# An encoder layer with expert-choice routing on one core: a half-width first gather, another order in the weight ring, and dummy matmuls

## The chip, the cores and the metric

The kernel runs on one NeuronCore of a Trainium2 chip. The metric is the device time of one execution in microseconds (us). Five engines work beside each other, each through its own queue and in order: TensorE (PE in the profile; PEld are its weight loads), VectorE (DVE), ScalarE (ACT), GpSimd (POOL) and SyncE (SP). SP issues nearly all DMA transfers here.

## What is computed

The reference is one layer of an encoder over 512 tokens of width 1024. Three token mixers (neighbourhood attention, grouped-query attention and attention to 256 memory tokens) are gated, added and normalized. Then comes a mixture of 16 experts, in which each expert chooses 64 tokens:

```python
cap = EC_CAPACITY_FACTOR * T // N_EXPERTS          # 64
aff = jax.nn.softmax(x @ w_router, axis=-1)
gate, idx = lax.top_k(jnp.swapaxes(aff, 1, 2), cap)
xs = x[bidx, idx]
h = jnp.einsum('becd,edf->becf', xs, w_gate_up)
hg, hu = jnp.split(h, 2, axis=-1)
ye = jnp.einsum('becf,efd->becd', jax.nn.silu(hg) * hu, w_down)
ye = ye * gate[..., None]
y = jnp.zeros_like(x).at[bidx, idx].add(ye)
out = layer_norm(DN_ALPHA * x + y, ln2_g, ln2_b)
```

All weights are float32. An expert has 12 MB of them, and each is used once.

## The kernel before, in words

The instructions of each engine stand in the order in which the Python code writes them; no scheduler moves them. A tile is allocated under a tag. The next tile of the same tag waits for the readers of the one before, also those written later.

**First half.** Weights of the mixers come in 74 units of 128 x 1024. Each is split into a high and a low part (`hi_lo`, L86 to L88: ScalarE rounds, VectorE subtracts), and three matmuls replace one. The first unit comes together with the memory tokens in four parts; `first_unit` (L288) does two high products of each part as soon as ScalarE is done, then four products with the low parts of VectorE. `k_item` (L308) calls it for h = 0 and then does the second unit in the same way (`t_piece`, L269 to L271: with k = 0 its third product is the first that needs the low part of the weights). Nine dummy matmuls on an identity (L234) run before.

**Routing.** After the last projection the router's logits are sorted per expert (`rounds`, L1093 and L1096), the cut is found (`cut`, `dg`, `thp` at L1170), positions come from `cnp` (L1179 to L1185). `keep_warm(n)` (L1113) issues n dummies; the call with 28 stands ahead of the sort's last part (L1156).

**Gather.** For a group of four experts, `onehot` (L1194) compares positions with 1 to 64 and gives a 512 x 256 one-hot (64 slots for each of the four experts). `gather` (L1208) multiplies the tokens, split in XH and XL, by it: for each of 8 feature blocks f, 8 matmuls with weights from XH or XL (L1216, L1218) and 256 moving columns, evacuated by VectorE (f even, L1223) or ScalarE (f odd, L1221). After the eighth step come the gate values gw (L1232) in the bank of tag Y, which has one buffer, and their reductions on VectorE (L1239). Before expert 0 three steps run, the others stand between the products of expert 0.

**Experts.** `gate_up` (L1245) multiplies the 64 gathered tokens by the two halves of a unit gu(e,k), k = 0 to 7; `h_transpose` (L1268) and `down` (L1277) use dn(e,k), k = 0 to 3. The loop over experts (L1526 on) does the first four gu of expert e, then dn of expert e-1, then the other four gu. In expert 2 `residual` (L1325) puts the tokens into the accumulator acc, in steps between the products: the first two steps, on VectorE (L1332), are written right after gu(2,0), four more (L1336, L1342) up to gu(2,2). Then comes the copy of hT(1) (L1275), without which the y product of expert 1 (L1287) can't start. acc has the tag G1.

**The ring.** A unit of expert weights has 1 MB. `RING` (L32) lists twelve blocks of one or two units, each in the buffer of a tag. `_blocks` (L40) puts the units, in the order of use, into blocks: first all twelve, then again and again the ten that are not in `ONCE` (raw and G1). Blocks 0 to 6 are loaded during the first half; blocks 7 to 9 (G1, Q6, Q9) wait for the last projection's operands, block 10 (M) for the token tile's last reader, block 11 (VS) for `cnp`. When the last unit of a block is used, `done` (L813) asks for the next block on SP's queue, whose request waits for TensorE's readers of that tag. Before the change Q6 holds dn(0,3) and gu(1,4), Q9 gu(1,5) and gu(1,6), M gu(1,7) and gu(2,0), VS gu(2,1), and G1 dn(0,1) and dn(0,2). Blocks 12 to 23 then go to Q2, Q1, Q5, Q7, Q4, Q3, Q6, Q9, M, VS, Q2, Q1; 23 follows in the buffer of dn(1,0) and dn(1,1).

Of the kernel before, what the change touches and what calls it, by code (L numbers as in the profile page):

```python
# [28 lines left out]
NEG = -1e30  # L29
RSQRT_SEED = float(0x5F3759DF)  # L30
N_UNITS = 74
RING = (("Q2", 2), ("Q1", 2), ("Q5", 2), ("Q7", 2), ("Q4", 2), ("Q3", 2), ("raw", 1), ("G1", 2), ("Q6", 2), ("Q9", 2), ("M", 2),  # L32
        ("VS", 1))
ONCE = ("raw", "G1")
N_SINGLE = 10
# [4 lines left out]
def _blocks():  # L40
    order = []
    for e in range(NEXP - 1):
        order += [("gu", e, k) for k in range(4)]
        if e:
            order += [("dn", e - 1, k) for k in range(4)]
        order += [("gu", e, k) for k in range(4, KD)]
    order += [("gu", NEXP - 1, k) for k in range(KD)]
    order += [("dn", e, k) for e in (NEXP - 2, NEXP - 1) for k in range(4)]
    again = [t for t in RING if t[0] not in ONCE]
    blocks, i = [], 0  # L50
    while i < len(order):
        b = len(blocks)
        tag, n = RING[b] if b < len(RING) else again[(b - len(RING)) % len(again)]
        blocks.append((tag, n, order[i:i + n], i + n > len(order) - N_SINGLE))
        i += n
    return blocks
# [3 lines left out]
def layer_kernel(ctx: ExitStack, tc: tile.TileContext, xt, xn, first0, wu, bgate, rpb, gains, wrt,  # L60
# [134 lines left out]
    def first_part(t, k, o, n):  # L195
        return t[:, k // 2, o + (k % 2) * n:o + (k % 2) * n + n]
# [81 lines left out]
    def n_chunk(acc, us, ah, al, m, hooks={}):  # L278
        c = slice(m * P, (m + 1) * P)
        for k in range(KD):  # L280
# [4 lines left out]
            nc.tensor.matmul(acc, ah[:, k, c], lo, start=False, stop=False)  # L285
            nc.tensor.matmul(acc, al[:, k, c], h, start=False, stop=(k == KD - 1))

    def first_unit(acc):  # L288
        for i in range(4):
            ks = (2 * i, 2 * i + 1)  # L290
            for k in ks:
                nc.tensor.matmul(acc, first_part(fh, k, 512, P), memh[:, k], start=(k == 0), stop=False)
            for k in ks:
                nc.tensor.matmul(acc, first_part(fh, k, 512, P), meml[:, k], start=False, stop=False)
                nc.tensor.matmul(acc, first_part(fl, k, 512, P), memh[:, k], start=False, stop=(k == KD - 1))
# [3 lines left out]
    def g_mem():  # L299
        zz = R("Q3", [P, 4, 1024], "mkvzs")  # L300
        ST["A5"] = zz[:, 0:2]
        ST["A6"] = zz[:, 2:4]
        mk = ST["A5"][:, 0].rearrange("p (h t) -> p h t", h=4)
        mv = ST["A6"][:, 0].rearrange("p (m f) -> p m f", m=2)
        qm = R("Q2", [P, 4, S], "qmT")
        ST.update(mkT=mk, mv=mv, qmT=qm)

        def k_item(h):  # L308
            u, = ws.take()
            ws.prefetch()  # L310
            acc = PB("mm", f"mk{h}")
            if h == 0:
                first_unit(acc[:, :256])
            else:
                t_unit(acc[:, :256], u, memh, meml)
            if h >= 2:
                split_x(h - 2)
            yield
            nc.vector.tensor_copy(mk[:, h], acc[:, :256])

        def q_item(h):
            u, = ws.take()
            ws.prefetch()
            acc = PB("mm", f"qm{h}")
            t_unit(acc, u, xh, xl)
            yield
            nc.scalar.activation(qm[:, h], acc, AF.Copy, scale=1.0 / math.sqrt(128.0))

        def v_item(q):
            us = ws.take(2)  # L330
            for m in range(2):
                acc = PB("mm", f"mv{q}{m}")
                n_chunk(acc[:, :256], us, memh, meml, m)
                ws.prefetch(1 + m)
                if q == 0:
                    split_x(2 + m)
                yield
                nc.scalar.copy(mv[:, m, q * 256:(q + 1) * 256], acc[:, :256])

        for h in range(4):  # L340
            yield from k_item(h)
        for q in range(2):
            yield from v_item(q)
        for h in range(4):
            yield from q_item(h)
# [807 lines left out]
    for m in (2, 3):  # L1153
        x1_norm(m)
        x1_parts(m)
    keep_warm(28)  # L1156
    ring.upto(len(RING))
    dump("aff", aff)

# [31 lines left out]

    OH, XS, GW = {}, {}, {}

    def onehot(qd):  # L1194
        OH[qd] = oh = R("oh", [P, NT, 256], f"oh{qd}", F16)
        for m in range(NT):
            nc.vector.tensor_tensor(oh[:, m].rearrange("p (e s) -> p e s", e=4),
                                    iota_t[:, None, :].to_broadcast([P, 4, CAP]),
                                    pos[:, m, 4 * qd:4 * qd + 4, None].to_broadcast([P, 4, CAP]), op=ALU.is_equal)

    def split_aff():
        a, b = (R("t", [P, NT * NEXP], n, bufs=2).rearrange("p (m e) -> p m e", m=NT) for n in ("affs", "affr"))
# [2 lines left out]
        nc.scalar.copy(aff3[:, :, :, 1], a)  # L1205
        nc.vector.scalar_tensor_tensor(aff3[:, :, :, 2], a, 1.0, aff3[:, :, :, 1], op0=ALU.mult, op1=ALU.subtract)

    def gather(qd):  # L1208
        oh = OH[qd]
        xs = [R("hi", [P, 4, 256], f"xs{qd}{j}", bufs=2) for j in range(2)]  # L1210
        XS[qd] = xs
        for f in range(KD):
            g = PB("mm", f"ga{qd}{f}")[:, :256]
            c = slice(f * P, (f + 1) * P)
            for m in range(NT):
                nc.tensor.matmul(g, XH[:, m, c], oh[:, m], start=(m == 0), stop=False)  # L1216
            for m in range(NT):
                nc.tensor.matmul(g, XL[:, m, c], oh[:, m], start=False, stop=(m == NT - 1))  # L1218
            dst = xs[f // 4][:, f % 4]
            if f % 2:  # L1220
                nc.scalar.activation(dst, g, AF.Identity, bias=lnT[:, 1, f:f + 1], scale=gT[:, f:f + 1])  # L1221
            else:
                nc.vector.tensor_scalar(dst, g, gT[:, f:f + 1], lnT[:, 1, f:f + 1], op0=ALU.mult, op1=ALU.add)  # L1223
            yield
        if qd == 0:
            split_aff()
        GW[qd] = gw = small([P, 4], "gw", bufs=2)
        gp2 = PB("Y", f"gw{qd}").rearrange("p (i c) -> p i c", i=2)
        for i in range(0, 4, 2):
            gp = gp2[:, i // 2]  # L1230
            for m in range(NT):
                nc.tensor.matmul(gp[:, 0:6], oh[:, m, i * CAP:(i + 2) * CAP],  # L1232
                                 aff3[:, m, 4 * qd + i:4 * qd + i + 2].rearrange("p e a -> p (e a)"),
                                 start=(m == 0), stop=(m == NT - 1))
        for i in range(0, 4, 2):
            gp = gp2[:, i // 2]
            for j in range(2):
                for b in (0, 64):
                    nc.vector.tensor_reduce(gw[b:b + 64, i + j:i + j + 1], gp[j * 64:j * 64 + 64, 3 * j:3 * j + 3],  # L1239
                                            axis=AX.X, op=ALU.add)  # L1240
        nc.vector.tensor_scalar(gw, gw, 0.5 / A_SCALE, None, op0=ALU.mult)

    GU, HT, YP = {}, {}, {}

# [274 lines left out]
            finish(m, 0)  # L1519
            finish(m, 1)  # L1520

    onehot(0)
    g0 = gather(0)
    steps(g0, g0, g0)
    side = iter(())
    for e in range(NEXP):  # L1526
        if e == 0:
            for k in range(KD):
                gate_up(0, (k,))
                steps(g0)  # L1530
            all_of(g0)
        elif e < NEXP - 1:
            if e == 2:
                side = residual()
            elif e == 3:
                side = combine(0)
            if e == 12:
                g2 = R("G0", [P, D], "ln2g")
                nc.scalar.copy(ident_r, ident)
                side = rows_of_norm(g2)  # L1540
            for k in range(4):
                if k == 3:
                    h_transpose(e - 1)
                gate_up(e, (k,))
                steps(side, side)
            if e % 2 or e == 12:
                all_of(side)
            down(e - 1)
            if e % 2:
                slots_T(e // 2)  # L1550
            if e % 4 == 3:
                onehot(e // 4 + 1)
            for k in range(4, KD):
                gate_up(e, (k,))
                if e == 2:
                    steps(side, side)
                elif e % 2 == 0 and k > 4:
                    if k == 5:
                        side = combine(e // 2 - 1)
                    steps(side, side, side)  # L1560
            all_of(side)
        else:
            sizes = dict(RING)
            pair, one = sorted(ring.free_at_end[:2], key=lambda t: -sizes[t])
            ap12 = R(pair, [P, 2, 2, NT, 256], "accp12", F32R)
            split_acc(1, ap12[:, 0])
            split_acc(2, ap12[:, 1])
            gate_up(e, range(4))
            x0 = [PB(b, f"xq0{mp}", (P, 2, 256)) for mp, b in enumerate("ST")]
            h_transpose(e - 1)  # L1570
            slots_T(e // 2)
            split_acc(3, R(one, [P, 2, NT, 256], "accp3", F32R))
            gate_up(e, (4, 5))
            x1q = preload(1, ("mm", "mm"))
            gate_up(e, (6, 7))
            spare = PB("mm", "spare")
# [152 lines left out]
```

## Time and profile before

| | us |
|---|---|
| runs (three) | 977.21, 979.08, 1060.49; median 979.08 |
| the profiled execution | 977.92 |
| its span, first to last instruction | 976.1 |
| TensorE busy | 944.4 |
| VectorE busy | 451.9 |
| ScalarE busy | 274.3 |

The time of the profiled execution is that of the whole program; the span holds only the instructions, so 1.8 us lie around it. A matmul's busy time overlaps that of the next, so starts rather than durations give the price of one in a row. Rows of groups have the line, the engine, the operation, the tiles (written <- read) and the count; "[0.93 <-ACT dg L1168]" is idle time ahead of an instruction and what ended it. In the chain of waits a row has its start, its length, and what the end of the program waited for in that time.

### The profile page before, as it was taken

To read this page: it belongs to the slowest core of one execution; us is meant where nothing else is said; L and a number is where in the kernel's file an instruction comes from. 1 tells how busy PE (TensorE), PEld (TensorE's weight loads), DVE (VectorE), ACT (ScalarE), POOL (GpSimd) and SP (SyncE) were. 2 spreads that over 40 slices of the span, in tenths; PEclk is the share of its full clock that TensorE was granted. 3 is DMA by queue.
4 is the path that set the end of the run, shared out by engine and by line. 5 is a ranking of instruction groups with operands and counts; after the bars stand their busy time and mean duration, and the time that the engine had idled before them with its cause. 6 is when DMAs were issued, how large, how long until landed. Compare 5 with 4: busy or idle time off the path is not lost.

```text
span 976.1 us, 13068 instructions
## 1 busy us (share of the span) xinstructions
PE 944.4 (97%) x5350; PEld 615.0 (63%) x5350; DVE 451.9 (46%) x857; ACT 274.3 (28%) x540; POOL 78.4 (8%) x86
## 2 busy tenths in 40 slices
PE   8999899999999999999999999999999998997996
PEld 8899787889888888887886333433343332432344
DVE  6347678765376566237464155331332222231426
ACT  5343345444354454323223000100010000100123
POOL 0002403000032231000013000000000000000003
PEclk9999999999999999999999999999999999999998
DMA  9312121111333322584719999999999999999992
GB/s 357 111 68 65 65 65 44 65 44 58 85 117 111 101 82 75 217 325 183 279 50 389 389 422 430 430 433 429 429 430 430 430 430 431 432 429 431 428 419 100
DMA packets 38473, 251.62 MB, mean 258 GB/s; under 512 B 12543, under 2 KB 12927, under 8 KB 24590
## 3 DMA queue, kind: packets, MB, share of 16 engines
q1 hardware_dynamic: 37982, 249.74, 63.5%
q10 hardware_dynamic: 432, 1.05, 0.3%
q8 instruction: 42, 0.69, 0.3%
q14 instruction: 17, 0.14, 0.0%
HBM read 247.89 MB, written 2.10 MB: 256 GB/s over the span
## 4 chain that ended last, share of the span: by engine, by line
PE 70%; DMA 18%; DVE 6%; ACT 2%; POOL 2%; issue 1%; SPq 0%; DVEq 0%; POOLq 0%; ACTq 0%
DMA w<-in_wx 17%; PE g L1254 7%; PE u L1254 7%; PE y L1287 6%; PE gate L269 4%; PE gate L271 4%; PE gate L270 4%; PE nqk L271 1%; PE nqk L270 1%; PE nqk L269 1%; PE gy L627 1%; PE pr L269 1%; PE pr L270 1%; PE pr L271 1%; PE ga L1216 1%
## 5 line engine op out<-in xcount | busy, mean ns | idle before, releaser
L1254 PE MATMUL g<-w,xs 128*64 128x512 f32 x512 | 134.7, 604 | 7.5 <-DMA w<-in_wx 7.5
L1254 PE MATMUL u<-w,xs 128*64 128x512 f32 x512 | 131.6, 592 | 0.0
L1287 PE MATMUL y<-w,hT 128*64 128x512 f32 x480 | 107.0, 594 | 4.6 <-DMA w<-in_wx 3.9
L87 ACT CAST y<-y 64x512 fp32r<-64x512 f32 x30 | 17.4, 579 | 240.3 <-PE y L1287 229.0
L88 DVE TENSOR_TENSOR y<-y,y 64x512 fp32r<-64x512 f32 x30 | 20.7, 689 | 135.2 <-ACT y L87 135.2
L1254 PEld LDWEIGHTS u<-w,xs 128*64 128x64 f32 x512 | 36.8, 137 | 73.1 <-issue 71.7
L1287 PEld LDWEIGHTS y<-w,hT 128*64 128x64 f32 x480 | 33.7, 137 | 74.4 <-issue 63.4
L88 DVE TENSOR_TENSOR los<-raw_twin,whi 128x1024 fp32r<-128x1024 f32 x43 | 54.0, 1257 | 51.3 <-ACT whi L87 51.0
L271 PE MATMUL gate<-xh,los 128*128 128x512 f32 x192 | 74.8, 390 | 0.0
L1254 PEld LDWEIGHTS g<-w,xs 128*64 128x64 f32 x512 | 31.3, 136 | 63.7 <-issue 48.0
L269 PE MATMUL gate<-xh,whi 128*128 128x512 f32 x160 | 63.6, 398 | 0.0
L270 PE MATMUL gate<-xl,whi 128*128 128x512 f32 x160 | 62.4, 390 | 0.0
L1357 DVE TENSOR_TENSOR acc<-acc,cb 128x512 f32<-128x512 f32 x56 | 35.4, 683 | 34.5 <-PE cb L1355 34.5
L87 ACT CAST whi<-raw_twin 128x1024 fp32r<-128x1024 f32 x43 | 45.2, 1051 | 7.3 <-PE wo L1062 4.4
L88 DVE TENSOR_TENSOR los<-raw_twin,los 128x1024 fp32r<-128x1024 f32 x21 | 27.4, 1305 | 36.6 <-ACT los L87 36.5
L1426 POOL TENSOR_TENSOR acc<-acc,ln2g 128x512 f32<-128x512 f32 x6 | 7.6, 1279 | 435.4 <-issue 433.4
L271 PEld LDWEIGHTS gate<-xh,los 128*128 128x128 f32 x192 | 36.1, 188 | 7.7
L603 ACT ACTIVATE att_twin<-gs,nm 128x512 f32<-128x512 f32 x32 | 21.7, 683 | 51.4 <-DVE nm L602 51.4
L1264 ACT ACTIVATE tg<-g 128x512 f32<-128x512 f32 x16 | 9.6, 597 | 94.0 <-PE g L1254 94.0
L1275 DVE COPY hT<-ht 128x512 f32<-128x512 f32 x15 | 10.4, 690 | 54.6 <-PE ht L1272 54.6
L269 PEld LDWEIGHTS gate<-xh,whi 128*128 128x128 f32 x160 | 30.0, 188 | 7.5 <-issue 1.0
L270 PEld LDWEIGHTS gate<-xl,whi 128*128 128x128 f32 x160 | 30.1, 188 | 5.9
(405 smaller groups left out, 1883.9 us busy)
## 6 DMA issues: line engine op xcount, KB each, us to landing
w<-in_wx SPq DMA_DIRECT2D x86, 2048.0 KB
raw_twin<-in_wu SPq DMA_DIRECT2D x65, 512.0 KB
w<-in_wx SPq DMA_DIRECT2D x20, 1024.0 KB
raw<-in_wu SPq DMA_DIRECT2D x8, 512.0 KB
xr<-in_xt SPq DMA_DIRECT2D x4, 512.0 KB
macc<-in_xn SPq DMA_DIRECT2D x2, 1024.0 KB
first<-in_first SPq DMA_DIRECT2D x4, 384.0 KB
bf<-in_rpb SPq DMA_DIRECT2D x64, 24.0 KB
```

Source lines behind the costliest of these rows:

```text
L87: nc.scalar.copy(hi, src)
L88: nc.vector.tensor_tensor(lo, src, hi.bitcast(F32), op=ALU.subtract)
L269: nc.tensor.matmul(acc, w_h, rh[:, k], start=(k == 0), stop=False)
L270: nc.tensor.matmul(acc, w_h, rl[:, k], start=False, stop=False)
L271: nc.tensor.matmul(acc, w_l, rh[:, k], start=False, stop=(k == nk - 1))
L603: nc.scalar.activation(self.p[:, h], self.s[h], AF.Exp, bias=nm[:, h:h + 1], accum_out=self.sm[:, h:h + 1])
L627: nc.tensor.matmul(self.y[h * 64:h * 64 + 64, :P], ST["vg"][:, kc, kvh * 64:kvh * 64 + 64], self.pt[:, h, kc], start=(kc == 0), stop=(kc = ...
L1216: nc.tensor.matmul(g, XH[:, m, c], oh[:, m], start=(m == 0), stop=False)
L1254: nc.tensor.matmul(GU[e][b][hf * 64:hf * 64 + 64], xs, w[b][:, hf * 512:hf * 512 + 512], start=(k == 0), stop=(k == KD - 1))
L1275: nc.vector.tensor_copy(t, tp)
L1287: nc.tensor.matmul(y[o * 64:o * 64 + 64], hT[:, c, hf * 64:hf * 64 + 64], w[j][:, o * 512:(o + 1) * 512], start=(k == 0 and j == 0), stop= ...
L1357: nc.vector.tensor_tensor(a, a, cb, op=ALU.add)
```

## The change

The first gather is made in two halves of 128 slots: experts 0 and 1 before and during expert 0, experts 2 and 3 between the first four gate-up products of expert 1. In the ring's first round G1 moves behind Q6 and Q9, and its two places take the last two units of that round, gu(2,0) and gu(2,1); the other units move up. So Q6 holds dn(0,1) and dn(0,2), Q9 dn(0,3) and gu(1,4), G1 gu(2,0) and gu(2,1), M gu(1,5) and gu(1,6), VS gu(1,7). From block 12 on nothing changes in tags or units. `first_unit` gets 12 dummies and the call behind it 5; the longest `keep_warm` gets 3 more. VectorE's second one-hot stands behind the first evacuation. Nothing else moves on any queue. SP issues as many transfers of the same sizes; blocks 7 to 9 go to Q6, Q9 and G1 instead of G1, Q6 and Q9.

```diff
-RING = (... ("raw", 1), ("G1", 2), ("Q6", 2), ("Q9", 2), ("M", 2), ("VS", 1))
+RING = (... ("raw", 1), ("Q6", 2), ("Q9", 2), ("G1", 2), ("M", 2), ("VS", 1))
...
     order += [("dn", e, k) for e in (NEXP - 2, NEXP - 1) for k in range(4)]
+    g = sum(n for _, n in RING[:[t for t, _ in RING].index("G1")])
+    last = sum(n for _, n in RING)
+    order[g:last] = order[last - 2:last] + order[g:last - 2]
...
+    def spin(n):
+        for _ in range(n):
+            nc.tensor.matmul(warm[:, :P], ident, ident, start=True, stop=True)
+
     def first_unit(acc):
         for i in range(4):
             ks = (2 * i, 2 * i + 1)
+            spin(1)
             for k in ks:
                 nc.tensor.matmul(acc, first_part(fh, k, 512, P), memh[:, k], start=(k == 0), stop=False)
+            spin(2)
             for k in ks:
...
                 first_unit(acc[:, :256])
+                spin(5)
...
-    keep_warm(28)
+    keep_warm(31)
     ring.upto(len(RING))
...
-    def gather(qd):
+    def gather(qd, e0=0, n=4):
...
-            g = PB("mm", f"ga{qd}{f}")[:, :256]
+            g = PB("mm", f"ga{qd}{f}")[:, :n * CAP]
...
-                nc.tensor.matmul(g, XH[:, m, c], oh[:, m], start=(m == 0), stop=False)
+                nc.tensor.matmul(g, XH[:, m, c], oh[:, m, sl], start=(m == 0), stop=False)
...
-        gp2 = PB("Y", f"gw{qd}").rearrange("p (i c) -> p i c", i=2)
-        for i in range(0, 4, 2):
+        gp2 = PB("Y", f"gw{qd}{e0}").rearrange("p (i c) -> p i c", i=2)
+        pairs = range(e0, e0 + n, 2)
+        for i in pairs:
...
-    onehot(0)
-    g0 = gather(0)
-    steps(g0, g0, g0)
+    onehot(0, 0, 2)
+    g0 = gather(0, 0, 2)
+    steps(g0, g0)
+    onehot(0, 2, 2)
+    g1 = gather(0, 2, 2)
...
                 gate_up(e, (k,))
                 steps(side, side)
+                if e == 1:
+                    steps(g1, g1)
+            if e == 1:
+                all_of(g1)
             if e % 2 or e == 12:
                 all_of(side)
             down(e - 1)
```

More of the change, by code (lines that the diff above doesn't have):

```diff
@@ L31 @@
 N_UNITS = 74
-RING = (("Q2", 2), ("Q1", 2), ("Q5", 2), ("Q7", 2), ("Q4", 2), ("Q3", 2), ("raw", 1), ("G1", 2), ("Q6", 2), ("Q9", 2), ("M", 2),
+RING = (("Q2", 2), ("Q1", 2), ("Q5", 2), ("Q7", 2), ("Q4", 2), ("Q3", 2), ("raw", 1), ("Q6", 2), ("Q9", 2), ("G1", 2), ("M", 2),
         ("VS", 1))
@@ L1192, in layer_kernel, with onehot @@
     OH, XS, GW = {}, {}, {}
-    def onehot(qd):
-        OH[qd] = oh = R("oh", [P, NT, 256], f"oh{qd}", F16)
+    def onehot(qd, e0=0, n=4):
+        if e0 == 0:
+            OH[qd] = R("oh", [P, NT, 256], f"oh{qd}", F16)
+        oh = OH[qd][:, :, e0 * CAP:(e0 + n) * CAP]
         for m in range(NT):
-            nc.vector.tensor_tensor(oh[:, m].rearrange("p (e s) -> p e s", e=4),
-                                    iota_t[:, None, :].to_broadcast([P, 4, CAP]),
-                                    pos[:, m, 4 * qd:4 * qd + 4, None].to_broadcast([P, 4, CAP]), op=ALU.is_equal)
+            nc.vector.tensor_tensor(oh[:, m].rearrange("p (e s) -> p e s", e=n),
+                                    iota_t[:, None, :].to_broadcast([P, n, CAP]),
+                                    pos[:, m, 4 * qd + e0:4 * qd + e0 + n, None].to_broadcast([P, n, CAP]), op=ALU.is_equal)
     def split_aff():
@@ L1206, in split_aff @@
         nc.vector.scalar_tensor_tensor(aff3[:, :, :, 2], a, 1.0, aff3[:, :, :, 1], op0=ALU.mult, op1=ALU.subtract)
-    def gather(qd):
+    def gather(qd, e0=0, n=4):
         oh = OH[qd]
-        xs = [R("hi", [P, 4, 256], f"xs{qd}{j}", bufs=2) for j in range(2)]
-        XS[qd] = xs
+        if e0 == 0:
+            XS[qd] = [R("hi", [P, 4, 256], f"xs{qd}{j}", bufs=2) for j in range(2)]
+            GW[qd] = small([P, 4], "gw", bufs=2)
+        xs, gw = XS[qd], GW[qd]
+        sl = slice(e0 * CAP, (e0 + n) * CAP)
         for f in range(KD):
-            g = PB("mm", f"ga{qd}{f}")[:, :256]
+            g = PB("mm", f"ga{qd}{f}")[:, :n * CAP]
             c = slice(f * P, (f + 1) * P)
             for m in range(NT):
-                nc.tensor.matmul(g, XH[:, m, c], oh[:, m], start=(m == 0), stop=False)
+                nc.tensor.matmul(g, XH[:, m, c], oh[:, m, sl], start=(m == 0), stop=False)
             for m in range(NT):
-                nc.tensor.matmul(g, XL[:, m, c], oh[:, m], start=False, stop=(m == NT - 1))
-            dst = xs[f // 4][:, f % 4]
+                nc.tensor.matmul(g, XL[:, m, c], oh[:, m, sl], start=False, stop=(m == NT - 1))
+            dst = xs[f // 4][:, f % 4, sl]
             if f % 2:
@@ L1224, in gather @@
             yield
-        if qd == 0:
+        if qd == 0 and e0 == 0:
             split_aff()
-        GW[qd] = gw = small([P, 4], "gw", bufs=2)
-        gp2 = PB("Y", f"gw{qd}").rearrange("p (i c) -> p i c", i=2)
-        for i in range(0, 4, 2):
+        gp2 = PB("Y", f"gw{qd}{e0}").rearrange("p (i c) -> p i c", i=2)
+        pairs = range(e0, e0 + n, 2)
+        for i in pairs:
             gp = gp2[:, i // 2]
@@ L1234, in gather @@
                                  start=(m == 0), stop=(m == NT - 1))
-        for i in range(0, 4, 2):
+        for i in pairs:
             gp = gp2[:, i // 2]
@@ L1240, in gather @@
                                             axis=AX.X, op=ALU.add)
-        nc.vector.tensor_scalar(gw, gw, 0.5 / A_SCALE, None, op0=ALU.mult)
+        gs = gw[:, e0:e0 + n]
+        nc.vector.tensor_scalar(gs, gs, 0.5 / A_SCALE, None, op0=ALU.mult)
     GU, HT, YP = {}, {}, {}
```

## The prediction

> **What bounds the kernel now.** I read the page first, then the chain of waits, then the stretch around the first gather in the timeline, and last the busy time by stretch.
>
> ```profile
> span 976.1 us, 13068 instructions
> PE   8999899999999999999999999999999998997996
> GB/s 357 111 68 65 65 65 44 65 44 58 85 117 111 101 82 75 217 325 183 279 50 389 389 422 430 430 433 429 429 430 430 430 430 431 432 429 431 428 419 100
> w<-in_wx SPq DMA_DIRECT2D x86, 2048.0 KB
> ```
> ```profile
> 778.67 36.36 DMA w<-in_wx
> ...
> 924.76 21.97 DMA w<-in_wx
> 946.86 1.98 PE yq L1405 x32
> ```
>
> Two regimes follow each other. In the first half TensorE is busy 0.8 or more of every slice and DMA is mostly idle. In the second half the expert weights come at 430 GB/s until 946.7 us (924.76 + 21.97), and from 778.67 to there the chain is DMA alone. After the last weights a tail of 976.1 - 946.7 = 29.4 us follows that the change leaves alone. So the end is: the time at which the weights start to stream, plus their bytes, plus every stretch in which the stream stands, plus the tail. A 2048 KB pair (2.097 MB) takes 2.097/0.430 = 4.88 us.
>
> ```profile
> 509.00:512.00 3.00, 2.59 (x23) 1.00 0.97 328
> 512.00:531.00 19.00, 17.79 (x153) 0.91 1.00 426
> 531.00:536.00 5.00, 5.00 (x32) 1.00 0.71 247
> 536.00:568.00 32.00, 32.00 (x166) 1.00 0.99 393
> 568.00:760.00 192.00, 191.24 (x948) 1.00 1.01 430
> ```
>
> The columns are the stretch, its length, TensorE's busy time, the granted clock, the DMA share and GB/s. Against 430 the stream loses 2.1 us (5 x 183/430) and then 2.8 us (32 x 37/430): 4.9 us, all before 568. **At most these 4.9 us can be won in the ring.** They are lost because the SP queue waits for TensorE to free a pair:
>
> ```profile
> 508.05 1.28 SPq L795 DMA_DIRECT2D w<-in_wx  x3
> 532.40 0.33 SPq L795 DMA_DIRECT2D w<-in_wx  x1
> 564.32 0.33 SPq L795 DMA_DIRECT2D w<-in_wx  x1
> 577.88 0.33 SPq L795 DMA_DIRECT2D w<-in_wx  x1
> 582.29 0.33 SPq L795 DMA_DIRECT2D w<-in_wx  x1
> ```
>
> Blocks 7 to 11 (9.44 MB) are asked for from 508.05 on. By 531 the rows above have moved 0.98 + 8.09 MB, so they are through at 531.8. Block 12, asked for at 532.40, follows 2.1 us late, at 533.9: 1.5 us from request to flow. An unbroken stream would want block 18 at 531.8 + 6 x 4.88 = 561.1 and block 23 at 531.8 + 10 x 4.88 + 2.44 = 583.0 (block 21 is a single unit). The lateness of a request is its time + 1.5 less that place. Block 18 (564.32) is 4.7 us late, block 23 (582.29) 0.8 us. The largest lateness is the whole loss, and 4.7 agrees with the 4.9 us above: **today block 18 decides**.
>
> **The change part by part.** *First gather.* The steps before and between the first gate-up products are on TensorE's path:
>
> ```profile
> 527.64 1.01 PE g L1254 x4
> 528.65 0.86 PE u L1254 x4
> 529.51 0.54 PE ga L1216 x4
> 530.05 0.44 PE ga L1218 x4
> ...
> 543.74 0.29 PE gw L1232 x8
> ...
> 555.22 6.87 PE y L1287 x32
> 562.09 0.33 PE gT L1307 x4
> ```
>
> A gather step of 256 slots costs 0.98 us, 0.11 per matmul. 128-slot f16 matmuls with a new weight each are not in this stage; nearest is gT, four of 128 columns in 0.33 us with the break, which leaves (0.33 - 0.10)/4 = 0.058 each. I take 0.56 us for a half step, and 0.46 for one that follows another. Bounds: 0.053 (half of 0.107) and 0.098, the weight load alone (below).
>
> From 527.64 to y(0) at 555.22 stand five steps (4.9 us) and 0.29 of gw. After, six half steps stand in expert 0 (3.4 us) with 0.25 of gw. Expert 1's first four products get the other half: four pairs of 1.02 us (4.1), some 0.45 for breaks, and a second gw. That gw is new on the path: its bank is the only Y bank, and y(0) takes it next, so TensorE waits for its four reductions.
>
> ```profile
> 544.07 1.36 DVE L1239 TENSOR_REDUCE gw<-gw 64x1 f32<-64x3 f32 x8 [0.50 <-PE gw L1232]
> ```
>
> Four of eight are 0.68 us; with the matmuls, their drain and the signals 1.1. So y(0) comes 27.6 - 5.2 + 3.65 + 4.1 + 0.45 + 1.1 = 31.7, with the uneven starts about 32.1 us after the first product. VectorE and ScalarE evacuate half tiles beside it at no cost; the second one-hot fits between two evacuations.
>
> *Start of the gather.* Two half steps instead of three full ones precede the first product. The clock matters here:
>
> ```profile
> 520.59 0.39 PE L1170 MATMUL thp<-dg,rt 16*128 16x16 f32 x2 [0.93 <-ACT dg L1168]
> 522.00:523.00 1.00, 1.00 (x21) 0.76 0.99 426
> 523.00:526.00 3.00, 3.00 (x16) 0.51 1.01 418
> 522.23 1.80 PE L1113 MATMUL warm<-ident 128*128 128x128 f32 x8
> 522.99 1.43 DVE L1197 TENSOR_TENSOR oh<-iota_t,rt 128x256 f16<-128x256 f32 x4
> ```
>
> The granted clock falls to half for some 3.4 us right after a stretch in which TensorE stood 0.93 us. The three more dummies (0.23 us each, below: 0.69) go into that 0.93 us and delay nothing. [...] Whether 0.69 us is enough no row shows; I take it to be. Then the dummies end at 523.3, the narrower one-hots (under 1.0 us for four) at 523.9, two half steps make the first product start at about 524.65 instead of 527.64. With the half clock it is 524.03 + 2 x 0.86 = 525.8.
>
> So y(0) starts at 556.75, 1.5 us later than before; at half clock 2.7 later. Block 12 is free at 524.65 + 4.3 = 529.0 instead of 532.40; blocks 12 to 16 are early enough for the stream.
>
> *Ring.* G1 is not lent again. With gu(2,0), gu(2,1) in it, block 18's buffer (Q6) holds dn(0,1), dn(0,2) and is free three quarters through y(0), at 556.75 + 5.2 = 561.95, lateness 2.4 instead of 4.7. The three loads asked for at 508.05 only change places. But the accumulator now waits for gu(2,1), and VectorE's queue stands behind it:
>
> ```profile
> 570.72 2.35 DVE L1332 TENSOR_TENSOR acc<-xhl 128x1024 f32<-128x1024 f16 x2
> 571.84 1.03 PE L1254 MATMUL u<-w,xs 128*64 128x512 f32 x4
> 577.87 0.68 DVE L1275 COPY hT<-ht 128x512 f32<-128x512 f32 x1
> 578.60 6.66 PE L1287 MATMUL y<-w,hT 128*64 128x512 f32 x30 [0.76 <-DVE hT L1275]
> ```
>
> Six accumulator operations (three pairs of 2.35) stand ahead of the copy of hT(1), and y(1) already waits 0.76 us for it. gu(2,1) ends at 572.87 (u of 571.84 and its 1.03), 2.15 after 570.72. So y(1) comes 1.5 + 2.15 = 3.7 us later, and block 23, freed by half of y(1), at 585.95 instead of 582.29. Its lateness becomes 585.95 + 1.5 - 583.0 = 4.4 us. Block 22 (577.88 + 1.5) is at 2.7, block 24 (3.4 of y after 23, against 4.88 of stream) at 3.0. **The stream stands 4.4 us instead of 4.7: -0.3.** At half clock it is 5.6, +0.9.
>
> *Dummies at the start.*
>
> ```profile
> 1.35 4.21 PE L234 MATMUL warm<-ident 128*128 128x128 f32 x18 [1.35 <-POOL ident masks.py:199]
> 9.10 0.50 PE L292 MATMUL mk<-firsth 128*128 128x256 f32 x2 [0.48 <-ACT firsth L87]
> 11.95 0.38 PE L271 MATMUL mk<-firsth,los 128*128 128x256 f32 x1 [0.88 <-DVE los L88]
> 13.00:32.00 19.00, 19.00 (x161) 1.00 0.76 296
> 513.25 6.41 PE L1113 MATMUL warm<-ident 128*128 128x128 f32 x56
> ```
>
> A dummy is two records: 0.43 us at the start (nine by 5.21), 0.229 later. A product is 19/161 = 0.118. Until 7 us there is time for one dummy, two products and two dummies; then 14 dummies (3.2) and 22 products (2.6) reach 12.8, and the second unit's third product comes at 13.0 instead of 11.95: +1.06 us. The waits of 0.48 and 0.88 us are filled, but 17 dummies are more than they hold. From 13 to 32 us TensorE has no idle time, so all of it stays. Lower bound 0, upper 1.5 (dummies slower for longer).
>
> Sum: +1.06 - 0.3 = +0.75 us. The profiled execution took 977.92 us (span 976.1), 1.2 below the median of the three runs, 979.08. **Forecast 978.7 us.**
>
> **The rivals.**
> [...]
> 2. *The accumulator's wait is covered*: if y(1) comes early enough, block 22 decides with 2.7 (-2.0) and the start costs nothing: 975.9. Against it: six operations of 1.18 us are in one queue.
> 3. *Slower: half-width matmuls bound by their weight load.*
> ```profile
> L1218 PEld LDWEIGHTS <-xhl 128*128 128x128 f16 x32 | 3.3, 104 | 0.6
> ```
> A load takes 0.10 us, hidden today under 0.107 of matmul. If it doesn't overlap a matmul of 0.055, 128 of them cost 0.04 more, 5.1 us by block 23: 983.8. Each 0.01 us of spacing costs 1.3 us, so it decides from about 0.06 on, where it takes back the ring's 0.3. Against it: gT's 0.058. [...]
> 4. *The change does nothing*: start hidden, ring as before: 977.9.
>
> **How the numbers follow.** Forecast 0.40; half clock 0.20; wait covered 0.22; weight loads 0.10; nothing 0.05; else 0.03. Runs of before differ by 0.9 us either way. The range 975.0 to 982.0 takes in rival 2 less that, and the half clock with half of rival 3; about 0.15 is left out. 2% (19.6 us, about what a measurement can tell from no change) is beyond every case: at most 4.9 us can be won, and the dearest rival costs 6. Faster 0.01, within 0.97, slower 0.02.
>
> **What would show it.** Right: the third product of the second unit at about 13.0; granted clock 1.0 from 522 to 526; first product near 524.7 plus that shift; no GB/s dip at 531 to 536; a dip near 580 to 590, with TensorE idle some 3 us before y(1) on hT. Wrong: a half step over 0.6 us, no idle time before y(1), or a start as early as before.

## The result, and the profile after

| | before | after |
|---|---|---|
| median of the runs (us) | 978.34 | 981.94 |
| lowest to highest | 977.21 to 979.63 | 981.06 to 983.25 |
| profiled execution, its span (us) | 977.92, 976.1 | 982.81, 980.9 |
| last down product starts (us) | 946.86 | 951.70 |

The ratio is 1.0033 (95% interval 1.0022 to 1.0044): by it the changed kernel is 3.2 us slower, and the medians differ by 3.6. It was put beside the kernel before a second time (E11 below): 1.0028 (1.0020 to 1.0037). One run of before at 1060.49 us was disturbed and is left out of the table. The forecast was 0.75 us more than the profiled execution, 978.7, in effect no change.

The page of the profile after:

```profile
span 980.9 us, 13289 instructions
GB/s 356 111 67 65 65 53 55 66 43 49 86 122 112 101 81 77 221 321 187 268 61 423 414 388 400 420 415 429 432 429 431 430 431 431 429 429 434 426 411 93
```
```profile
951.70 1.98 PE yq L1421 x32
```

The last line is from the chain of waits: the last product of the experts starts 951.70 - 946.86 = 4.84 us later than before. The span grew by 4.8, so the tail behind it is unchanged. In the GB/s row before, the stream was thin at the start (389, 389, 422) and then steady at 430. Now the start is better (423, 414) and the thin slices come later (388, 400, 420, 415). The busy time by stretch of after says where:

```profile
531.00:536.00 5.00, 5.00 (x37) 2.03 (x36) 0.41 (x1) 0.46 (x1) 0.00 (x0) 1.00 1.02 428
536.00:568.00 32.00, 31.19 (x214) 13.38 (x214) 7.64 (x22) 5.59 (x12) 0.00 (x0) 1.00 0.98 403
568.00:588.00 20.00, 17.33 (x74) 5.40 (x70) 11.19 (x11) 0.60 (x1) 0.00 (x0) 0.92 0.98 407
588.00:600.00 12.00, 12.00 (x56) 3.98 (x54) 6.34 (x7) 1.75 (x3) 0.00 (x0) 0.99 0.86 345
568.00:760.00 192.00, 189.33 (x934) 74.63 (x928) 65.51 (x110) 18.58 (x32) 0.00 (x0) 0.99 0.99 419
```

The columns are the stretch, its length, the busy time of PE, PEld, DVE, ACT and POOL, the granted clock, the DMA share and GB/s. The gap at 531 to 536 is closed (428 instead of 247), and 568 to 760, where before ran at 430, now loses 192 x 11/430 = 4.9 us. The SP queue's requests of after, blocks 7 (with 8 and 9), 12, 18, 22, 23 and 33, taken from the timeline:

```profile
509.88 1.28 SPq L805 DMA_DIRECT2D w<-in_wx  x3
531.11 0.33 SPq L805 DMA_DIRECT2D w<-in_wx  x1
563.28 0.33 SPq L805 DMA_DIRECT2D w<-in_wx  x1
580.76 0.33 SPq L805 DMA_DIRECT2D w<-in_wx  x1
588.78 0.33 SPq L805 DMA_DIRECT2D w<-in_wx  x1
635.65 0.33 SPq L805 DMA_DIRECT2D w<-in_wx  x1
```

Before they were at 508.05, 532.40, 564.32, 577.88, 582.29 and, for block 33, here:

```profile
629.17 0.33 SPq L795 DMA_DIRECT2D w<-in_wx  x1
```

So the first half ends 1.83 us later (509.88 against 508.05). Blocks 12 and 18 come earlier all the same, and from block 23 to block 33 the requests are 6.5 us late. What lies ahead of block 23 is y(1); after's VectorE and TensorE there:

```profile
575.85 2.36 DVE L1348 TENSOR_TENSOR acc<-xhl 128x1024 f32<-128x1024 f16 x2 [2.17 <-PE u L1270]
578.13 2.34 DVE L1352 SCALAR_TENSOR_TENSOR acc<-acc,r1g 128x1024 f32<-128x1024 f32 x2
580.39 2.34 DVE L1358 SCALAR_TENSOR_TENSOR acc<-r1b,acc 128x1024 f32<-128x1024 f32 x2
582.66 0.68 DVE L1291 COPY hT<-ht 128x512 f32<-128x512 f32 x1
```
```profile
556.82 0.24 PE L1247 MATMUL gw<-aff,oh 128*128 128x6 f16 x4
557.88 7.09 PE L1303 MATMUL y<-w,hT 128*64 128x512 f32 x32 [0.81 <-PE gw L1247]
578.20 0.66 PE L1288 MATMUL ht<-ident,h 128*128 128x128 f32 x4
579.69 1.03 PE L1270 MATMUL u<-w,xs 128*64 128x512 f32 x4
583.39 8.78 PE L1303 MATMUL y<-w,hT 128*64 128x512 f32 x32 [2.67 <-DVE hT L1291]
```

VectorE stands 2.17 us for gu(2,1), and its six accumulator operations are ahead of the copy of hT(1). TensorE stands 2.67 us instead of 0.76. Then y(1) takes 8.78 us instead of about 7: the granted clock is at half for 3.41 us from 584.76 on. A second such stretch lies at 100 us, where before had none; it makes most of the first half's 1.83 us. Two rows of after, then before's:

```profile
96.00:100.00 4.00, 2.19 (x14) 1.54 (x13) 3.37 (x9) 2.47 (x7) 0.00 (x0) 1.00 0.00 0
100.00:104.00 4.00, 4.00 (x22) 4.00 (x22) 3.40 (x9) 1.72 (x7) 0.00 (x0) 0.57 0.00 0
```
```profile
100.00:104.00 4.00, 4.00 (x37) 4.00 (x36) 3.41 (x11) 1.55 (x6) 0.00 (x0) 1.00 0.00 0
```

### The profile page after: what moved, and what is told of

It reads as the page before. It is cut to its first block, busy times and chain, and to the rows that moved or that the text cites. A ratio compares the mean times of both kernels' runs of the same rounds, so it can differ in the third digit from the quotient of the medians.

```text
span 980.9 us, 13289 instructions
## 1 busy us (share of the span) xinstructions
PE 950.5 (97%) x5454; PEld 620.9 (63%) x5454; DVE 453.7 (46%) x866; ACT 276.0 (28%) x544; POOL 78.6 (8%) x86
## 3 DMA queue, kind: packets, MB, share of 16 engines
q10 hardware_dynamic: 432, 1.05, 0.3%
## 4 chain that ended last, share of the span: by engine, by line
PE 70%; DMA 17%; DVE 7%; ACT 2%; POOL 2%; issue 2%; DVEq 0%; POOLq 0%; SPq 0%; ACTq 0%
DMA w<-in_wx 17%; PE g L1270 7%; PE u L1270 7%; PE y L1303 7%; PE gate L272 4%; PE gate L273 4%; PE gate L274 4%; PE nqk L272 1%; PE nqk L274 1%; PE nqk L273 1%; PE gy L637 1%; PE pr L272 1%; PE pr L273 1%; PE pr L274 1%; PE ga L1231 1%
```

## The experiments

Each ratio is to the kernel before on the same chip, with its 95% interval. E1 to E4 ran on one chip, E5 to E8 on a second, E9 to E11 on a third, so kernels of different sets are compared by their ratios. "End" is the start of the last down product in the profiled execution (before 946.86).

| | kernel | ratio | median (us) | end (us) |
|---|---|---|---|---|
| E1 | after, no start dummies | 1.0020 (1.0011 to 1.0029) | 979.88 | 948.90 |
| E2 | before, start dummies | 1.0006 (0.9997 to 1.0014) | 978.57 | 947.94 |
| E3 | after, old ring order | 1.0015 (1.0007 to 1.0024) | 980.04 | 949.03 |
| E4 | after, all residual steps behind hT(1) | 1.0002 (0.9993 to 1.0010) | 978.71 | 946.66 |
| E5 | after, eight steps right behind hT(1) | 0.9993 (0.9984 to 1.0001) | 977.19 | 945.65 |
| E6 | E5 and late gw | 0.9985 (0.9976 to 0.9994) | 976.67 | 944.87 |
| E7 | E6, no start dummies | 0.9977 (0.9965 to 0.9989) | 976.17 | 946.51 |
| E8 | before, new ring order | 1.0014 (1.0002 to 1.0026) | 979.97 | 948.03 |
| E9 | after, wait before y(1) filled | 1.0021 (1.0011 to 1.0030) | 980.55 | 948.68 |
| E10 | E8, eight steps behind hT(1) | 0.9994 (0.9984 to 1.0003) | 977.60 | 945.98 |
| E11 | after once more | 1.0028 (1.0020 to 1.0037) | 980.75 | 949.08 |

**E1 and E2: the start dummies, taken out of after and put alone into before.**

```diff
-            spin(1)
...
-            spin(2)
...
-                spin(5)
```

> The changed kernel without the 17 start dummies; nothing else is undone. Theory A (the dummies lie 0.35 us deep on TensorE's path, and by moving the work behind them they also bring a half-clock window of 3.41 us at 100 us, which costs another 1.5): 981.9 - 1.85 = 980.1 us, no window of lower clock near 100 us, and block 7 of the ring asked for near 508.0. Theory B (the window at 100 us came by chance of the one execution that was profiled): 981.9 - 0.35 = 981.6. The term of the prediction, 1.06 us: 980.9.

> The kernel before with the 17 start dummies alone. Theory A (0.35 us on the path and the window at 100 us with its 1.5): 978.7 + 1.85 = 980.6 us, block 7 asked for near 509.9. Theory B (no window that belongs to the dummies): 979.05. The term of the prediction, 1.06 us: 979.8.

Taken alone, E1 looks like theory A (979.88; A had 980.1). E2 and the other runs speak against it. E2 costs 0.6 us (-0.3 to +1.4), not 1.9, and neither E1 nor E2 has a stretch of half clock at 100 us (the eight `my` matmuls there take 1.05 us in both, 1.75 in after). But E3, E4, E5, E6 and E9, which keep the dummies, have none either, and E7, without them, has one. So it doesn't come with the dummies, and theory A falls. What they cost depends on when TensorE turns fast at the start; the first record of a full granted clock is at 7.11 us in before's trace and at 4.49 in after's. In E2 a pair of dummies takes 0.63 us at 5.35 and 0.38 at 7.58:

```profile
5.35 0.63 PE L290 MATMUL warm<-ident 128*128 128x128 f32 x2
7.58 0.38 PE L290 MATMUL warm<-ident 128*128 128x128 f32 x2
13.07 0.29 PE L271 MATMUL mk<-firsth,los 128*128 128x256 f32 x1
```

and in E4 0.39 from the first, at 5.29:

```profile
5.29 0.39 PE L293 MATMUL warm<-ident 128*128 128x128 f32 x2
12.16 0.28 PE L274 MATMUL mk<-firsth,los 128*128 128x256 f32 x1
```

The third product of the second unit starts at 13.07 and 12.16, against 11.95 before: 1.1 or 0.2 us. From there to the first request of the ring the profiled executions without a half-clock stretch at 100 us take 496.0 to 496.1 us (496.10 in before, 496.00 in E4), so it is not won back. Without dummies it isn't 11.95 always: in E1 it was 12.41. Over all profiled executions that product starts at 11.84 on average without the dummies (five of them) and at 12.45 with them (eight), 0.6 us later. The ratios say 0.6 (E2) to 0.8 us (E11 less E1: 0.0028 - 0.0020 of 978).

**E3, E8, E10: the ring order.** E3 puts the old order into after. E8 puts the new one into before, with no gather in halves and no dummies:

```diff
-RING = (... ("raw", 1), ("G1", 2), ("Q6", 2), ("Q9", 2), ("M", 2), ("VS", 1))
+RING = (... ("raw", 1), ("Q6", 2), ("Q9", 2), ("G1", 2), ("M", 2), ("VS", 1))
...
+    g = sum(n for _, n in RING[:[t for t, _ in RING].index("G1")])
+    last = sum(n for _, n in RING)
+    order[g:last] = order[last - 2:last] + order[g:last - 2]
```

> The changed kernel with the ring order of before: half gather and start dummies stay. Theory A (the accumulator waits for the second load in its own buffer, VectorE's queue waits behind it, and that delays y(1)): y(1) starts no later than 1 us after TensorE's last work ahead of it, the stream loses nothing at block 23; in its place block 18 is asked for near 567.0 and is 5.5 us late, as far as the first half's shift and the later y(0) push it. Time 981.3. Theory B (y(1) is late because of the half gather itself, not the ring): y(1) waits as in the changed kernel and block 18 is late as well: 984 or more.

> The kernel before with the new ring order alone: no half gather, no dummies. By the prediction's steps block 18's buffer is free three quarters through y(0), near 560.5, and no longer late by 4.7; in exchange the accumulator waits for the second load of its own buffer and y(1) waits some 2 us longer on hT, block 23 is asked for near 584.5, 3.0 us late: the stream stands 3.0 instead of 4.7, 978.0 - 1.7 = 976.3. Theory B (the accumulator's wait costs what the ring gains, also through TensorE's later time at block 33): 977.5 to 979. Theory C (the ring order is what costs the changed kernel its 3 us, whatever the gather): over 979.

E3's request for block 18, its y(1) and its stretch behind it:

```profile
565.96 0.33 SPq L802 DMA_DIRECT2D w<-in_wx  x1
```
```profile
580.23 7.09 PE L1300 MATMUL y<-w,hT 128*64 128x512 f32 x32 [0.76 <-DVE hT L1288]
```
```profile
588.00:600.00 12.00, 12.00 (x54) 4.11 (x51) 8.70 (x10) 1.18 (x2) 0.00 (x0) 1.00 1.00 430
```

The trace is as theory A has it: y(1) waits 0.76 us again, nothing is lost at block 23, and block 18 is late (565.96; its first half ended 1.3 us earlier than the expectation took it). The time, 980.04, is lower than the 981.3 that I had. It is 1.5 us above that of before, where after's is 3: the new order doesn't pay in the changed kernel. E8 points the same way for the kernel before. Its requests for blocks 18 and 23, and y(1):

```profile
559.24 0.33 SPq L798 DMA_DIRECT2D w<-in_wx  x1
584.65 0.33 SPq L798 DMA_DIRECT2D w<-in_wx  x1
```
```profile
579.34 8.70 PE L1290 MATMUL y<-w,hT 128*64 128x512 f32 x32 [2.67 <-DVE hT L1278]
```

Block 18 comes 1.3 us earlier than the prediction's steps put it (560.5) and block 23 where they put it (584.5), though y(1) ahead of it has half clock (0.57 granted from 579 to 583), which those steps don't have. The time rises by 1.4 us (0.2 to 2.5) where they promised 1.7 less. The wait of 2.67 us is there without any half gather. E8's timed runs also have a lower mean granted clock than those of before beside them, 0.9940 against 0.9956; 0.0016 of 978 us is 1.6 us of clock, so how much of the 1.4 us is the ring's is not settled.

**E4 and E5: the accumulator's steps moved behind the copy of hT(1).** E4 issues no step before the fourth product of expert 2, then two, then three a product; E5 issues eight at once behind the copy and leaves four. This is E5's edit:

```diff
-                steps(side, side)
+                if e != 2:
+                    steps(side, side)
+                elif k == 3:
+                    steps(*[side] * 8)
```

> The changed kernel with the accumulator's steps begun behind the transposes of h(1) (two at the fourth product of expert 2, then three a product instead of two): the copy of hT(1) has nothing of the accumulator ahead of it on VectorE. Theory A (the accumulator's wait delays that copy by some 2 us, and the idle time brings the half clock into y(1), 1.9 more): the wait of y(1) on hT falls under 1 us, no half-clock window in y(1), TensorE some 4 us earlier, and of the stream's loss after 588 us (2.8 at block 23, 1.5 near 636) all is won: 977.6 us. Theory B (TensorE is late there by its work, the half-clock window is bound to no wait): less than 1.5 us is won, 980.5 to 982. Theory C (the steps behind the product delay the evacuation of y(1) or the gate of expert 2): no gain, 982 or more.

> The changed kernel with eight of the accumulator's twelve steps issued right behind the copy of hT(1) instead of two a product ahead of it; the other four stand where the kernel before has them. It answers why the first try at this (all steps after the copy) kept only 0.6 us of the 1.9 us by which its stream led at 588 us. Theory A (that try lost 3.5 us of TensorE at 593 to 605, because ten of the twelve steps came after y(1) and TensorE then waited for VectorE; that made block 33 late): here VectorE does eight steps while TensorE does y(1), TensorE has no wait over 1 us between 588 and 605, block 33 is asked for before 630 and the stream keeps its lead of about 1.9 us: 978.0 - 1.9 = 976.1 (975.5 to 977). Theory B (block 33 is late for the half gather's own TensorE time, about 1 us of weight loads and a wait): no better than the first try, 978.0 to 979.

E4 wins the wait and 3 us of time, but less than hoped. y(1) has no wait and starts at 578.05, 5.3 us earlier (1.7 of them from the first half), and then:

```profile
588.00:600.00 12.00, 10.85 (x48) 3.46 (x44) 11.89 (x12) 0.60 (x1) 0.00 (x0) 1.00 0.99 425
632.00:636.00 4.00, 4.00 (x22) 1.36 (x20) 0.00 (x0) 0.00 (x0) 0.00 (x0) 1.00 0.88 303
```

VectorE is busy 11.89 of 12 us, TensorE waits 1.15 us for acc at 597 and 0.99 at 601, and block 33 is asked for at 632.01. The stream breaks at 632 to 636. In E5 VectorE does eight steps during y(1):

```profile
588.00:600.00 12.00, 12.00 (x52) 4.36 (x53) 8.77 (x11) 0.73 (x2) 0.00 (x0) 1.00 1.00 430
632.00:636.00 4.00, 4.00 (x22) 1.48 (x20) 0.69 (x1) 0.00 (x0) 0.00 (x0) 1.00 1.02 426
```

Block 33 is asked for at 629.65 and the gap is gone; the end is 1.0 us earlier than in E4, and the time 977.19. The mechanism of theory A shows in both: the wait goes, and in E5 the late block 33 too. Both times are about 1.1 us above what I had (977.6 and 976.1), and E5's lies between its two theories.

> The kernel before with the new ring order and with eight of the accumulator's steps right behind the copy of hT(1); no half gather, no dummies. Theory A (the ring order alone was eaten by the accumulator's wait at block 23, 1.3 us of stream, and by the half clock behind it): the stream keeps what the ring order wins at block 18, 0.8 to 0.9 us, and the time is 977.4. The rest up to the 976.7 to 977.2 of the changed kernel with the same order of steps is then what the half gather is worth. Theory B (the ring order gains nothing whatever VectorE does): 978.3 or more.

E10 is E8 with the same edit: 1.0014 becomes 0.9994. The accumulator's wait, with what follows from it, cost 2 us, more than the ring order wins. The gain that is left, 0.6 us, is not told from none. E5, which has the half gather and the start dummies besides, stands at 0.9993: what those two are worth together is not told from none either.

**E6 and E7: the second gate sums later, and then without start dummies.**

```diff
-            if e == 1:
-                all_of(g1)
...
                 gate_up(e, (k,))
+                if e == 1 and k == 6:
+                    all_of(g1)
```

> As the run before it in this set, and the second half's gate sums (gw) are taken at the seventh product of expert 1 instead of ahead of y(0), where TensorE waits for four reductions in the only Y bank. Theory A (that wait is on the path that frees block 18): y(0) starts 0.8 to 1.1 us earlier, block 18 is asked for near 560.6, and the time falls by about 1 us more: 975.2. Theory B (block 18 isn't the decider any more, or TensorE is the bound by then): same time as the run before it within 0.4 us.

> As the run before it in this set, without the 17 start dummies. Theory A (the dummies cost 0 to 1.1 us, by where the clock turns full between 4.4 and 7.1 us): 0.6 us less, 974.6. Theory B (they cost nothing on average): the same within 0.3 us.

In E6 y(0) has no wait of 0.81 us for the Y bank and starts 0.67 earlier than in E5, block 18 is asked for at 561.20 instead of 561.86, and the end moves from 945.65 to 944.87. The times differ by 0.5 us, within both intervals, and E6's 976.67 is above the 975.2 of its theory A. E7 has the lowest median seen here, and its ratio puts it 2.2 us under the kernel before (1.1 to 3.4); its interval overlaps E6's, so what it gains by leaving out the dummies is not shown. Its profiled execution holds a half-clock stretch at 99.5 us (0.64 granted from 100 to 104), so its end (946.51) is not its usual one.

**E9 and E11: the wait filled, and after once more.**

```diff
+                if e == 2 and k == 3:
+                    warm3 = PB("mm", "warm3")
+                    for _ in range(11):
+                        nc.tensor.matmul(warm3[:, :P], ident, ident, start=True, stop=True)
```

> The changed kernel with eleven dummy matmuls (0.23 us each, 2.5 us) between the fourth product of expert 2 and y(1), where TensorE stood 2.67 us on hT. Nothing else moves. Theory A (the half-clock window inside y(1), seen in two of three executions that had this wait, comes of the idle time): no window in y(1), which takes 6.9 us; y(1) starts no earlier, and the time falls by what the window costs on average, some 1.0 us: 980.3. Theory B (such windows come and go by their own timing, whatever TensorE does in the stretch ahead): the time stays that of the changed kernel, 981.3, and a window may still show in y(1). If the dummies end later than hT comes, y(1) starts later and the time rises.

> The changed kernel itself, beside the two others on the same chip, for two questions: its distance to the kernel before once more (1.0033 by the first comparison: 981.2 to 981.7), and which half-clock windows a second profiled execution of it has. Theory A (a window behind the wait of 2.67 us is usual, the one at 100 us is not): one in y(1), none at 100 us. Theory B (both belong to the changed kernel): both again. Theory C (both came by chance): neither.

In E11 the wait is the same 2.67 us, but y(1) runs at full clock (7.09 us); the half clock at 100 us is there again (0.57 granted from 100 to 104). So of four executions with the wait (after, E1, E8, E11) two have half clock behind it: y(1) takes 8.78 us in after and 8.70 in E8, 7.09 in E1 and E11. The mean granted clock of the timed runs says more than single profiles: 0.9947 in E11's eleven, 0.9966 in E9's twelve. The difference, 0.0019 of 978 us, is 1.9 us of lost clock, about one stretch of 3.41 us at half. The timed runs don't say where the stretches lay, and one at 100 us counts as well. Mean time fell by 0.6 us (981.09 against 980.46), and the intervals of the two ratios overlap. That the idle time brings the half clock is likely by this and by what the last section shows; that it costs 0.6 us is not shown.

E9 is also the cleanest look at the change, with no half clock before the tail. Its y(1), which starts no earlier; its requests for blocks 18, 23 and 33; its stretches; and the last two stretches in before:

```profile
581.81 7.09 PE L1303 MATMUL y<-w,hT 128*64 128x512 f32 x32
```
```profile
561.70 0.33 SPq L805 DMA_DIRECT2D w<-in_wx  x1
585.50 0.33 SPq L805 DMA_DIRECT2D w<-in_wx  x1
632.37 0.33 SPq L805 DMA_DIRECT2D w<-in_wx  x1
```
```profile
536.00:568.00 32.00, 31.19 (x210) 13.05 (x208) 7.64 (x22) 5.14 (x11) 0.00 (x0) 1.00 0.98 405
568.00:588.00 20.00, 19.98 (x104) 8.26 (x102) 11.19 (x11) 0.60 (x1) 0.00 (x0) 1.00 0.97 392
588.00:600.00 12.00, 12.00 (x56) 4.10 (x54) 8.45 (x10) 1.76 (x3) 0.00 (x0) 1.00 0.99 415
632.00:636.00 4.00, 4.00 (x21) 1.31 (x18) 0.07 (x1) 0.00 (x0) 0.00 (x0) 1.00 0.90 336
636.00:640.00 4.00, 4.00 (x22) 1.46 (x21) 0.69 (x1) 0.00 (x0) 0.00 (x0) 1.00 0.97 365
```
```profile
632.00:636.00 4.00, 4.00 (x22) 1.48 (x20) 0.69 (x1) 0.00 (x0) 0.00 (x0) 1.00 1.01 434
636.00:640.00 4.00, 4.00 (x21) 1.29 (x19) 0.00 (x0) 0.00 (x0) 0.00 (x0) 1.00 1.02 438
```

## Why the prediction was right or wrong

Most of the mechanisms were right, and the rule that made a loss of them was not: I forecast 0.75 us more, in effect no change, and the kernel is 2.7 to 3.2 us slower by the two ratios.

- *What bounds it*: right. The gap at 531 to 536 closed, and most of what was won and lost behind the ring's first request shows in its gaps (point 3 below has what doesn't).
- *Half step of the gather*: right. In after a step and its break take 0.55 us (528.58 to 529.13), one that follows another 0.45 (I had 0.56 and 0.46):

```profile
553.06 0.39 PE L1231 MATMUL ga<-oh,xhl 128*128 128x128 f16 x4
553.29 0.39 PE L1233 MATMUL ga<-oh,xhl 128*128 128x128 f16 x4
553.51 0.61 PE L1288 MATMUL ht<-ident,h 128*128 128x128 f32 x4
```

  The rival of the weight loads (983.8) falls: here a load and a matmul of 128 columns take 0.45/8 = 0.056 us.
- *First product, y(0), block 18*: right. In after less its first half's 1.83 us: 524.88 (I had 524.65), 556.05 (556.75), 561.45 (561.95). The gate sums' wait is 0.81 us. With the three more dummies the wait ahead of thp is 0.26 us instead of 0.93. That they hold the clock is not shown: E2, E8 and E10 have the old 28 and full clock there as well (1.00 from 512 to 531 in E8 and E10).
- *The accumulator's wait*: right as a wait, 1.9 us more on hT (I had 2.15), and block 23 at 585.50 in E9 (585.95). The rival that has this wait covered falls with it.
- ***"The stream stands 4.4 us instead of 4.7: -0.3"*: this step failed.** It rests on "the largest lateness is the whole loss", and that rule gave too little. In before it had agreed (4.7 for 4.9), and that one agreement was all that it rested on. In E9 the ring's first request is only 0.24 us later than before, and the end 1.82 later: 1.6 us more lost behind it, with no half clock in it. E9's time says 1.3 to 1.5 us more (0.0021 of 978 is 2.1, less 0.6 to 0.8 for the dummies). The gaps in its stretches add up to only 0.6 us more than those of before (point 3). So the stream lost 0.6 to 1.6 us more, not 0.3 less. Three things bear on it.
  1. My list of lateness ended at block 24. TensorE was late by 3 us from block 23 on, and block 33 had little to give. Its place is 531.8 + 19 x 4.88 + 2 x 2.44 = 629.4. Before, 629.17 + 1.5 is 1.3 late; in E9 632.37 + 1.5 is 4.5 late, more than block 23 (4.0), and the stream breaks once more at 632 to 640 (336 and 365 GB/s, before 434 and 438). E4 and E5 show it from the other side. By the rule alone, though, 4.5 would still be less than 4.7.
  2. The 4.7 us that I set against it held a half-clock stretch at 522 us which E2, E8 and E10 don't have. In E2 block 18 comes 564.65 - 509.08 = 55.6 us after block 7, in the profiled execution of before 56.3. By the rule that makes the exchange 4.4 for 4.0. The end doesn't show it: the last down product starts 438.86 us after block 7's request in E2 and 438.81 in before.
  3. The loss is not the largest lateness alone. From E9's stretches it is 32 x 25/430 = 1.9 (536 to 568, at 405 GB/s), 1.8, 0.4, 0.9 and 0.6, together 5.5 us before rounding, where before had 4.9, while no block is more than 4.5 late. E6 shows it more plainly. Its block 18 is the latest, at 561.20 + 1.5 against a place of 561.8 (561.1, and its first request is 0.7 later): 0.9 us. It loses 1.2 and 0.7 us all the same:

```profile
536.00:568.00 32.00, 32.00 (x210) 12.72 (x206) 6.85 (x17) 5.13 (x11) 0.00 (x0) 1.00 0.99 414
568.00:588.00 20.00, 20.00 (x96) 6.64 (x92) 12.86 (x18) 1.75 (x3) 0.00 (x0) 1.00 1.00 415
```

  So the gaps add up beyond the largest lateness. Why, and why E9's end moved 1 us more than its gaps, stays open.
- *Start dummies, +1.06*: right in sign, too large on average. It was 1.1 in E2 and 0.2 in E4; the averages are 0.6 to 0.8.
- *Half clock*: I looked for it at 522 us alone. It came behind the new wait of y(1), where it made 1.7 us of TensorE time in after (y(1) took 8.78 instead of 7.09), and at 100 us in both executions of after, 1.5 us in the first (509.88 - 12.30 = 497.6 us from the third product to the first request, 496.1 in before).

The 2.7 to 3.2 us are then: dummies 0.6 to 0.8, the stream's 1.3 to 1.6 by E9's time and end, and about 0.6 for half clock behind the wait, 2.5 to 3.0 together. The second and third are read from E9's time, so the sum is no test of its own; the third is not shown, and the second is only partly found in gaps. With E5's order of VectorE's queue the same change is no slower than before.

## What to carry to other kernels

Ask of each buffer that is lent to a stream who takes it next, and let nothing stand behind that taker in its engine's queue: eight operations issued a few lines later were worth 3.4 to 3.9 us here (E5 against after) and 2 us in the kernel before with the new ring order (E10 against E8), half clock included. When a wait makes an engine late, follow its lateness to the point where the stream's slack is smallest, which was ten blocks further on, and not only to the next request. Add up the gaps of a stream; the largest lateness alone said 0.9 us in E6, where the gaps were 1.9. An effect of 1 us needs timed rounds beside it, since one profiled execution may hold a stretch of half clock that the next does not.

## What was not expected of the hardware

The half-clock stretches last 3.41 us each in before and after (before 522.52 to 525.93; after 100.07 to 103.48 and 584.76 to 588.17), and they come and go between executions of one program: after has one inside y(1), E11, the same kernel, has none there. The wait of 1.81 us before the transposes at 99 us is in before, after, E1, E3, E7, E9 and E11 (before's and after's below), and three of them (after, E7, E11) have half clock behind it:

```profile
98.93 0.70 PE L563 MATMUL mt<-ident,att_twin 128*128 128x128 f32 x4 [1.81 <-DVE att_twin L536]
```
```profile
99.19 0.70 PE L573 MATMUL mt<-ident,att_twin 128*128 128x128 f32 x4 [1.81 <-DVE att_twin L546]
```

In both traces the changes of the granted clock ahead of the tail lie whole multiples of 3.413 us apart (before at 7.11, 522.52 and 525.93; after at 4.49, 100.07, 103.48, 584.76 and 588.17). Continued as a grid, an estimate from these times, they say where a wait lay. In after the wait at 99 us lies wholly inside one interval (96.65 to 100.07), and 2.04 of the 2.67 us ahead of y(1) lie in another (581.35 to 584.76). In before the 0.93 us ahead of `thp` lie in one (519.10 to 522.52). The clock falls at the end of each of the three. But in before the 1.81 us at 99 us lie wholly inside one too (95.85 to 99.26), and the clock stays full behind it (1.00 from 100 to 104). What makes the difference stays open.
